# Zero-filled 128-partition tiles for the 16-token block of a hybrid four-layer kernel

## The chip, the core and the metric

The kernel runs on one core of one Trainium2 chip. A core has five engines with instruction queues of their own: TensorE (PE; its weight loads are listed as PEld), VectorE (DVE), ScalarE (ACT), GpSimd (POOL) and SyncE (SP, which issues the transfers here). They share two memories of 128 partitions: SBUF for the data and PSUM, into which PE writes. The metric is the time of one execution in microseconds (us); lower is better.

## The reference

A sequence of 1040 tokens (16 learned "meta" tokens, then 1024 input tokens, each with 1024 features) goes through four layers: attention, mLSTM, HGRN2, attention. Each layer is

```python
u = rmsnorm(h, norm_gain[i])
y = branch(u, ...)          # attention (0, 3), mLSTM (1), HGRN2 (2)
h = h + where(valid, y, 0)
```

and the output is `h` without the meta tokens. The reference fills up the front to a whole block of 128 with tokens that are not valid, so its first block holds only the 16 meta tokens. The attention is causal within a window of 128 tokens, has 16 heads with 4 key/value heads, and a learned sink per head in its softmax. The other two branches are recurrences that carry a state per head from block to block:

```python
# mLSTM, a block of 128, per head (8 heads, keys of 128, values of 256)
qk  = (q @ k.T) * exp(D - m_t)
num = w_inter * (q @ C) + qk @ v
C   = w_old * C + (w_s * k).T @ v
# HGRN2, per head (8 heads, keys and values of 128)
o   = (q * exp(A)) @ S + att @ v
S   = exp(A_last) * S + (k * exp(A_last - A)).T @ v
```

All of it is float32.

## The kernel before

The tokens lie along the free dimension in most places (`x`, `uh`, `ul` are 128 features by 1040 tokens for each of eight feature groups). The padding of the reference is not computed: the sequence is cut into nine blocks, block 0 with the 16 meta tokens (`NMETA`) and eight of 128. Function `blk(b)` gives a block's first token and its length.

**The big projections.** A float32 product is made of three products of F32R tiles: a number is split into a high and a low part (`split`), and high by high, high by low and low by high are added up in PSUM. `proj` (line 231) makes projections with tokens in columns, in chunks of 400, 384 and 256 tokens; `proj_v` (lines 276 and 280) makes values with tokens in rows, a block at a time; `proj_out` (line 325) is the output projection. Beside these, each layer has a mixer made of small products, most of them plain float32 products, which PE executes in two passes (a group "x2" in the timeline).

**Layer 0 and 3, attention** (`layer_a`). The work is cut into units: four pairs of query tiles, nine blocks (eight in layer 3, where block 0 is not needed), two halves. A unit has three steps. `S_step` makes the scores on PE (lines 723, 724), puts the sinks behind them on POOL (line 728), and makes the softmax on DVE, ACT and POOL in tile `Sm` (lines 731 to 737). `T_step` transposes `Sm` on PE (line 749) and splits the result into `Ph` on ACT (line 751) and `Pl` on DVE (line 752). `V_step` multiplies by the values (line 768). The steps of one unit are put two units apart (`T_LAG`, `V_LAG`): in the order on PE, V_step of a unit, T_step of the unit two later and S_step of the one four later follow each other. `Sm`, `Ph` and `Pl` have two buffers each.

**Layer 1, mLSTM** (`layer_b`). Per head and block, `s1` makes the scores and the weighted keys (tiles `w`, `kw`, lines 997 and 1003), `s2` the output (line 1010, and from block 1 on line 1012 with the carried state), normalised into `hn` on ACT (line 1018), `s3` the update of the state (line 1024), and `s4` transposes `hn` (line 1038) back to tokens in columns. The values come from `put_v` (lines 243 to 246), which copies them from PSUM to a tile of 128x258; for block 0 it adds two parts, which `proj_v` left in rows 0 to 15 and 32 to 47. A column of ones stands behind the values (`g.memset` at line 972).

**Layer 2, HGRN2** (`layer_c`). Per head there are five regions: block 0 alone, then pairs of blocks. `level` and `level_mm` make the decayed scores (lines 1236 to 1262), `tail0` adds them up to `att`, `tail1` transposes the weighted keys (line 1312) into `kT` (line 1314), `states` updates the state (line 1322), `tail2` makes the output (lines 1343 and 1345).

In block 0 these products use 16 partitions: for instance `W["kw", b][:cn]` by `V[:cn, :257]` in `s3`, with `cn` = 16.

**What sets the order.** The order on PE is written out by hand: every layer makes lists of steps with a cost, `weave` mixes the list of a mixer with the list of projections in proportion to their costs, and the result is executed as listed. PE's order is thus the same whatever the other engines do. Their order is made by the framework: it takes the instructions as the program emits them, with the mixers' steps raised by 40 places (`hi`, `PRIO`), and lists them on each engine by priority and by the times that its own estimates give. It also sets the waits, and it gives a tile a buffer when the first instruction that touches it is listed.

The functions that the change touches, with the callers:

Of the kernel before, what the change touches and what calls it, by code (L numbers as in the profile page):

```python
# [15 lines left out]
P = 128  # L16
# [97 lines left out]
def hybrid_kernel(ctx: ExitStack, tc: tile.TileContext, ins, out, layers=(0, 1, 2, 3)):  # L114
# [125 lines left out]
    def put_v(V, acc, b, cn):  # L240

        if b == 0:
            s.copy(V[:cn, :256], acc[32 : 32 + cn, :256])
            v.tensor_tensor(V[:cn, :256], V[:cn, :256], acc[:cn, :256], op=ALU.add)
        else:
            s.copy(V[:cn, :256], acc[:cn, :256])
# [232 lines left out]
    def layer_a(i, j, first, last, fin, scale=None):  # L479
# [217 lines left out]
        def mixers():  # L697


            def S_step(w):  # L700
# [16 lines left out]
                S = psum("pm", 2).rearrange("p (u k) -> p u k", u=2)  # L717
                w["Sm"] = Sm = mix.tile([P, 2, 257], F32, tag="Sm", name=nm("Sm"), bufs=2)
                st, den = small(2), small(2)
                sinks = []  # L720
# [19 lines left out]
            def T_step(w):  # L740
# [4 lines left out]
                w["Ph"] = Ph = R["mix"].tile([P, 2, 2, P], F32R, tag="Ph", name=nm("Ph"), bufs=2)  # L745
                w["Pl"] = Pl = R["mix"].tile([P, 2, 2, P], F32R, tag="Pl", name=nm("Pl"), bufs=2)
                for ki, (kb, ko, _) in enumerate(kbs):
                    for u in range(2):
                        pe.transpose(pt[:kn, ki, u, :nq], Sm[:nq, u, ko : ko + kn], ident[:nq, :nq])  # L749
                src, h, l = (z[:kn, : len(kbs), :, :nq] for z in (pt, Ph, Pl))  # L750
# [3 lines left out]
            def V_step(w):  # L754
                b, kbs, hh, pair = w["b"], w["kbs"], w["hh"], w["pair"]
                q0, nq = blk(b)
                kn = NMETA if b == 0 else P
                grp = [z for z in GROUPS if b in z][0]
# [7 lines left out]
                for ki, (kb, _, _) in enumerate(kbs):  # L766
                    for part in ("Ph", "Pl"):
                        pe.matmul(po[:, :, q0 - g0 : q0 - g0 + nq], V[pair // 2, kb][:kn, P * hh : P * hh + P],  # L768
                                  w[part][:kn, ki, :, :nq], start=(ki == 0 and part == "Ph"),
                                  stop=(ki == len(kbs) - 1 and part == "Pl"))  # L770
# [87 lines left out]
    def layer_b(i, j, fin):  # L858
# [116 lines left out]
        def mixer(h):  # L975
# [8 lines left out]
            def s1(b):  # L984
# [10 lines left out]
                s.activation(E[:cn, :cn], E[:cn, :cn], AF.Exp)  # L995
                W["W", b] = w = mix.tile([P, P], F32, tag="W", name=nm("W"), bufs=2)
                v.tensor_tensor(w[:cn, :cn], E[:cn, :cn], pq[:cn, :cn], op=ALU.mult)
                if b:
                    W["qw", b] = qw = mix.tile([P, P], F32, tag="qw", name=nm("qw"), bufs=2)
                    v.tensor_tensor(qw, q[:, cs], R["wb"][:, cs], op=ALU.mult)  # L1000
                if b < NB - 1:
                    W["kw", b] = kw = mix.tile([P, P], F32, tag="kw", name=nm("kw"), bufs=2)
                    s.activation(kw[:cn], pq[:cn, 128:256], AF.Identity, scale=E[:cn, cn - 1 : cn])

            def s2(b):
# [3 lines left out]
                num = psum("po", 1)  # L1009
                pe.matmul(num[:cn, :257], W["W", b][:cn, :cn], V[:cn, :257], start=True, stop=(b == 0))  # L1010
                if b:
# [4 lines left out]
                v.reciprocal(den[:cn], den[:cn])  # L1016
                W["hn", b] = hn = mix.tile([P, 256], F32, tag="hn", name=nm("hn"), bufs=2)
                s.activation(hn[:cn], num[:cn, :256], AF.Identity, scale=den[:cn])

            def s3(b):  # L1020
                mix = R["mix"]
                c0, cn = blk(b)
                pc = psa()
                pe.matmul(pc[:, :257], W["kw", b][:cn], R["v", h, b][:cn, :257], start=True, stop=True)  # L1024
                Cn = mix.tile([P, 258], F32, tag="C", name=nm("C"), bufs=2)
# [7 lines left out]
            def s4(b):  # L1033
                c0, cn = blk(b)
                cs = slice(c0, c0 + cn)
                pt = psum("pt", 1)
                for c in range(2):
                    pe.transpose(pt[:, c * P : c * P + cn], W["hn", b][:cn, c * P : c * P + P], ident[:cn, :cn])
                for c in range(2):
                    v.tensor_copy(R["h", h, c][:, cs], pt[:, c * P : c * P + cn])  # L1040
# [90 lines left out]
    def layer_c(i, j, fin):  # L1131
# [80 lines left out]
        def mixer(h):  # L1212
# [56 lines left out]
            def tail0(r):  # L1269
# [10 lines left out]
                if r == 0:  # L1280
                    att = R["mix"].tile([16, 16], F32, tag="att0", name=nm("att0"), bufs=1)
                    v.tensor_reduce(att, t6[:16, 0, f0:, :w].rearrange("p l t -> p t l"),
                                    axis=mybir.AxisListType.X, op=ALU.add)
# [22 lines left out]
            def tail1(r):  # L1306
                c0, cn = geom(r)
                bn = min(cn, P)
                pt = psum("pt", 1)
                W["kT", r] = kT = R["mix"].tile([P, 256], F32, tag="kT", name=nm("kT"), bufs=1)  # L1310
                for b in range(len(REGIONS[r])):
                    pe.transpose(pt[:bn, P * b : P * b + P], W["kA", r][:, P * b : P * b + bn], ident)
# [3 lines left out]
            def states(r):  # L1316
# [3 lines left out]
                for b in blocks:  # L1320
                    cn = blk(REGIONS[r][b])[1]
                    pe.matmul(pc[:, P * b : P * b + P], W["kT", r][:cn, P * b : P * b + P],
                              R["v", h // 2, REGIONS[r][b]][:cn, vs], start=True, stop=True)
                for b in blocks:
# [7 lines left out]
            def tail2(r, b):  # L1332
# [9 lines left out]
                att = W["att", r] if r == 0 else W["att", r][:, b, :]  # L1342
                pe.matmul(W["po"][:, oc], V[:cn, vs], att, start=True, stop=(r == 0))
                if r:
# [263 lines left out]
```

## Time and profile before

| | |
|---|---|
| time, median of 3 runs | 2616.81 us (2613.16 to 2617.46) |
| the profiled execution: time | 2619.49 us |
| the profiled execution: span, first to last instruction | 2617.7 us |
| mean granted clock of PE in it | 0.993 |
| instructions | 54451 |
| DVE busy | 1961.7 us (75%) |
| ACT busy | 1696.7 us (65%) |
| POOL busy, instructions | 238.8 us (9%), 488 |

A view by line lists groups of equal instructions with their busy time and mean duration. The timeline lists single instructions in order of time: start, duration, engine, line, operation, the tile written and the tiles read, the shape. For PE the shape begins with the loaded weights: "16*128 16x257" means weights of 16 partitions by 128 columns and 257 columns streamed through 16 partitions. A bracket at the end names idle time of the engine before this instruction, and what ended it; "issue" is a wait for nothing that the profile shows. A view by windows gives the busy time of PE, PEld, DVE, ACT and POOL in stretches of the span, with the number of instructions in brackets. Matmuls overlap: the next one begins before the end of the one before, so their durations add up to more than the time that passes, and their starts are what to read.

### The profile page before, as it was taken

Reading aid. Unit: us, or ns where it says so; the run is one execution under the profiler, and the core shown is the slowest. Engines: PE = TensorE matmul, PEld = TensorE weight load, DVE = VectorE, ACT = ScalarE, POOL = GpSimd, SP = SyncE. Lnnn points to the kernel's source line nnn. Section 1 sums busy time; section 2 is a strip of 40 time slices with the busy share of each in tenths; the row PEclk is TensorE's granted clock in tenths of the full one; section 3 lists DMA queues with packets and bytes.
Section 4 is the critical chain, followed back from the end, with each engine's and each line's share of the span. In section 5 each row is a group of like instructions: output and inputs, shape, how many; then the busy total and the mean of one; then the engine's idle time right before and its main releaser. Section 6 shows DMA issues by size and latency. Waiting matters only on the chain.

```text
span 2617.7 us, 54451 instructions
## 1 busy us (share of the span) xinstructions
PE 2571.5 (98%) x20446; PEld 2493.2 (95%) x20446; DVE 1961.7 (75%) x5290; ACT 1696.7 (65%) x4434; POOL 238.8 (9%) x488
## 2 busy tenths in 40 slices
PE   8999999999999999999999999999999999999999
PEld 7899989999999999999999999999999999999999
DVE  6797888885747464646565688989887978887896
ACT  7766767575555555455545757878685857767772
POOL 0321221000000000000000000100000000321330
PEclk8999999999999999999999999999999999999999
DMA  4123112021111111111111101111110112212112
GB/s 149 53 67 98 54 54 71 21 67 57 41 58 41 50 44 53 41 57 41 55 43 50 53 30 42 34 34 34 34 42 30 38 51 88 59 47 84 55 41 77
DMA packets 86058, 140.21 MB, mean 54 GB/s; under 512 B 12425, under 2 KB 39186, under 8 KB 85794
## 3 DMA queue, kind: packets, MB, share of 16 engines
q1 hardware_dynamic: 85794, 136.73, 17.0%
q8 instruction: 161, 2.64, 0.4%
q14 instruction: 103, 0.84, 0.1%
HBM read 121.83 MB, written 4.27 MB: 48 GB/s over the span
## 4 chain that ended last, share of the span: by engine, by line
PE 75%; DVE 8%; ACT 4%; DMA 1%; issue 1%; POOL 0%; SPq 0%; DVEq 0%; ACTq 0%; POOLq 0%
PE pj L231 37%; PE pj L325 15%; PE pj L280 10%; PE po L768 1%; PE pt L749 1%; PE po L1010 1%; PE pa L1024 1%; PE po L1012 1%; PE pj L276 1%; PE pm L1262 1%; DVE wl L196 1%; PE pm L723 1%; DMA cs<-in_rope 1%; PE pm L724 1%; DVE Sm L731 1%
## 5 line engine op out<-in xcount | busy, mean ns | idle before, releaser
L231 PE MATMUL pj<-uh,wh 128*128 128x256 f32 (+2 forms) x2688 | 917.0, 341 | 7.2 <-ACT uh L400 6.7
L231 PE MATMUL pj<-ul,wh 128*128 128x256 f32 (+2 forms) x2688 | 866.5, 322 | 0.3
L231 PE MATMUL pj<-uh,wl 128*128 128x256 f32 (+2 forms) x2688 | 866.5, 322 | 0.0
L231 PEld LDWEIGHTS pj<-uh,wh 128*128 128x128 f32 x2688 | 510.1, 190 | 24.4 <-issue 9.3
L231 PEld LDWEIGHTS pj<-ul,wh 128*128 128x128 f32 x2688 | 510.6, 190 | 6.0 <-DVE ul L196 0.9
L231 PEld LDWEIGHTS pj<-uh,wl 128*128 128x128 f32 x2688 | 509.4, 190 | 0.0
L196 DVE TENSOR_TENSOR wl<-wr,wh 128x512 fp32r<-128x512 f32 (+1 forms) x338 | 232.5, 697 | 52.0 <-ACT wh L195 48.8
L195 ACT CAST wh<-wr 128x512 fp32r<-128x512 f32 (+1 forms) x338 | 202.7, 613 | 99.4 <-PE pj L325 33.4
L325 PE MATMUL pj<-yh,wh 128*128 128x384 f32 (+2 forms) x768 | 253.8, 330 | 9.9 <-DVE x L328 8.0
L328 DVE TENSOR_TENSOR x<-x,pj 128x384 f32<-128x384 f32 (+2 forms) x480 | 234.9, 509 | 33.3 <-PE pj L325 32.0
L325 PE MATMUL pj<-yh,wl 128*128 128x384 f32 (+2 forms) x768 | 246.2, 321 | 0.0
L325 PE MATMUL pj<-yl,wh 128*128 128x384 f32 (+2 forms) x768 | 246.1, 320 | 0.0
L280 PE MATMUL pj<-wh,uh 128*128 128x256 f32 (+1 forms) x768 | 232.7, 303 | 0.0
L280 PE MATMUL pj<-wl,uh 128*128 128x256 f32 (+1 forms) x768 | 216.4, 282 | 0.0
L280 PE MATMUL pj<-wh,ul 128*128 128x256 f32 (+1 forms) x768 | 216.0, 281 | 0.0
L734 ACT ACTIVATE Sm<-Sm,s 128x257 f32<-128x257 f32 (+2 forms) x272 | 130.9, 483 | 88.9 <-DVE s L731 84.5
L737 POOL TENSOR_TENSOR Sm<-Sm,s 128x512 f32<-128x512 f32 (+2 forms) x136 | 142.4, 1047 | 421.0 <-DVE s L736 407.4
L457 ACT ACTIVATE t<-t 128x384 f32<-128x384 f32 (+2 forms) x240 | 117.8, 491 | 82.3 <-DVE t L456 80.0
L325 PEld LDWEIGHTS pj<-yh,wh 128*128 128x128 f32 x768 | 144.9, 189 | 14.1 <-DVE x L328 9.7
L195 ACT CAST yh<-r 128x384 fp32r<-128x384 f32 (+2 forms) x120 | 56.9, 479 | 153.1 <-PE pj L325 136.9
L280 PEld LDWEIGHTS pj<-wh,uh 128*128 128x128 f32 x768 | 144.7, 188 | 2.2
L280 PEld LDWEIGHTS pj<-wl,uh 128*128 128x128 f32 x768 | 144.9, 189 | 1.9
(287 smaller groups left out, 5408.7 us busy)
## 6 DMA issues: line engine op xcount, KB each, us to landing
wr<-in_b_win SPq DMA_DIRECT2D x124, 256.0 KB, 3.0
wr<-in_a_win SPq DMA_DIRECT2D x80, 256.0 KB, 2.9
wr<-in_c_win SPq DMA_DIRECT2D x64, 256.0 KB, 2.7
wr<-in_a_wout SPq DMA_DIRECT2D x32, 256.0 KB, 2.9
wr<-in_b_wout SPq DMA_DIRECT2D x32, 256.0 KB, 2.8
t<-t SPq DMA_DIRECT2D x100, 48.0 KB, 2.0
cs<-in_rope SPq DMA_DIRECT2D x11, 400.0 KB, 3.4
cs<-in_rope SPq DMA_DIRECT2D x11, 384.0 KB, 3.7
```

Of the source, the lines that this page charges most:

```text
L195: s.copy(h, src)
L196: v.tensor_tensor(l, src, h.bitcast(F32), op=ALU.subtract)
L231: pe.matmul(acc[:, :cn], a[:, k, :], b[:, k, c0 : c0 + cn], start=(k == 0 and i == 0), stop=(k == KT - 1 and i == 2))
L276: pe.matmul(acc[:48, :nc], um[0][:, k, :], m[:, kk, :], start=(k == 0 and m is wh), stop=(k == KT - 1 and m is wl))
L280: pe.matmul(acc[:cn, :nc], a[:, k, c0 : c0 + cn], m[:, kk, :], start=(k == 0 and j == 0), stop=(k == KT - 1 and j == 2))
L325: pe.matmul(acc[:, :cn], a[:, k, mc], b, start=(k == 0 and i == 0), stop=(k == 1 and i == 2))
L328: v.tensor_tensor(x[:, m, c0 : c0 + cn], x[:, m, c0 : c0 + cn], acc[:, :cn], op=ALU.add)
L457: s.activation(a[:, :cn], a[:, :cn], AF.Exp)
L723: pe.matmul(S[:nq, u, :kw], q[:, qb], kh[:, kb], start=True, stop=False)
L724: pe.matmul(S[:nq, u, :kw], q[:, qb], kl[:, kb], start=False, stop=True)
L734: s.activation(Sm[:nq, u, : nk + 1], Sm[:nq, u, : nk + 1], AF.Exp, scale=-1.0, bias=st[:nq, u : u + 1], accum_out=den[:nq, u : u + 1])
L737: g.tensor_tensor(Sm[:nq, :, :nk], Sm[:nq, :, :nk], den[:nq].rearrange("p (u c) -> p u c", c=1).to_broadcast([nq, 2, nk]), op=ALU.mult)
```

## The change

For block 0, the tiles that feed the small products are filled with zeros by GpSimd before their 16 used partitions (or columns) are written, and the products then read all 128 partitions. These are `V` of layers B and C (in `put_v`), `Sm`, `Ph` and `Pl` of layer 0, `w`, `kw` and `hn` of layer B, and `att` and `kT` of layer C (`att` grows from 16 to 128 partitions). `V` of layer 0 had its zeros already (line 679). The transpositions of `Sm` and `hn` use the whole 128x128 identity, and so stream 128 columns in place of 16. The number of columns of the other products is unchanged; `W` in `s2` keeps its 16 columns of weights. The added rows are zeros, so the sums stay what they were.

```diff
     def put_v(V, acc, b, cn):
         if b == 0:
+            g.memset(V, 0.0)
             s.copy(V[:cn, :256], acc[32 : 32 + cn, :256])
...
                 w["Sm"] = Sm = mix.tile([P, 2, 257], F32, tag="Sm", name=nm("Sm"), bufs=2)
+                if b == 0:
+                    g.memset(Sm[:, :, :NMETA], 0.0)
...
+                if b == 0:
+                    for z in (Ph, Pl):
+                        g.memset(z[:, 0, :, :NMETA].bitcast(F32), 0.0)
                 for ki, (kb, ko, _) in enumerate(kbs):
                     for u in range(2):
-                        pe.transpose(pt[:kn, ki, u, :nq], Sm[:nq, u, ko : ko + kn], ident[:nq, :nq])
+                        pe.transpose(pt[:kn, ki, u, :], Sm[:, u, ko : ko + kn], ident)
...
-                        pe.matmul(po[:, :, q0 - g0 : q0 - g0 + nq], V[pair // 2, kb][:kn, P * hh : P * hh + P],
-                                  w[part][:kn, ki, :, :nq], start=(ki == 0 and part == "Ph"),
+                        pe.matmul(po[:, :, q0 - g0 : q0 - g0 + nq], V[pair // 2, kb][:, P * hh : P * hh + P],
+                                  w[part][:, ki, :, :nq], start=(ki == 0 and part == "Ph"),
...
                 W["W", b] = w = mix.tile([P, P], F32, tag="W", name=nm("W"), bufs=2)
+                if b == 0:
+                    g.memset(w[:, :cn], 0.0)
...
                     W["kw", b] = kw = mix.tile([P, P], F32, tag="kw", name=nm("kw"), bufs=2)
+                    if b == 0:
+                        g.memset(kw, 0.0)
...
-                pe.matmul(num[:cn, :257], W["W", b][:cn, :cn], V[:cn, :257], start=True, stop=(b == 0))
+                pe.matmul(num[:cn, :257], W["W", b][:, :cn], V[:, :257], start=True, stop=(b == 0))
...
                 W["hn", b] = hn = mix.tile([P, 256], F32, tag="hn", name=nm("hn"), bufs=2)
+                if b == 0:
+                    g.memset(hn, 0.0)
...
-                pe.matmul(pc[:, :257], W["kw", b][:cn], R["v", h, b][:cn, :257], start=True, stop=True)
+                pe.matmul(pc[:, :257], W["kw", b], R["v", h, b][:, :257], start=True, stop=True)
...
-                    pe.transpose(pt[:, c * P : c * P + cn], W["hn", b][:cn, c * P : c * P + P], ident[:cn, :cn])
+                    pe.transpose(pt[:, c * P : c * P + P], W["hn", b][:, c * P : c * P + P], ident)
...
-                    att = R["mix"].tile([16, 16], F32, tag="att0", name=nm("att0"), bufs=1)
-                    v.tensor_reduce(att, t6[:16, 0, f0:, :w].rearrange("p l t -> p t l"),
+                    att = R["mix"].tile([P, 16], F32, tag="att0", name=nm("att0"), bufs=1)
+                    g.memset(att, 0.0)
+                    v.tensor_reduce(att[:16], t6[:16, 0, f0:, :w].rearrange("p l t -> p t l"),
...
                 W["kT", r] = kT = R["mix"].tile([P, 256], F32, tag="kT", name=nm("kT"), bufs=1)
+                if r == 0:
+                    g.memset(kT[:, :P], 0.0)
...
-                    pe.matmul(pc[:, P * b : P * b + P], W["kT", r][:cn, P * b : P * b + P],
-                              R["v", h // 2, REGIONS[r][b]][:cn, vs], start=True, stop=True)
+                    pe.matmul(pc[:, P * b : P * b + P], W["kT", r][:, P * b : P * b + P],
+                              R["v", h // 2, REGIONS[r][b]][:, vs], start=True, stop=True)
...
-                pe.matmul(W["po"][:, oc], V[:cn, vs], att, start=True, stop=(r == 0))
+                pe.matmul(W["po"][:, oc], V[:, vs], att, start=True, stop=(r == 0))
```

More of the change, by code (lines that the diff above doesn't have):

```diff
@@ L756, in V_step @@
                 q0, nq = blk(b)
-                kn = NMETA if b == 0 else P
                 grp = [z for z in GROUPS if b in z][0]
```

## The prediction

> **What bounds the kernel now.** I read the page first: the busy line, then the chain that ended last.
>
> ```profile
> span 2617.7 us, 54451 instructions
> PE 2571.5 (98%) x20446; PEld 2493.2 (95%) x20446; DVE 1961.7 (75%) x5290; ACT 1696.7 (65%) x4434; POOL 238.8 (9%) x488
> PE 75%; DVE 8%; ACT 4%; DMA 1%; issue 1%; POOL 0%; SPq 0%; DVEq 0%; ACTq 0%; POOLq 0%
> ```
>
> PE is busy 98% of the span and carries 75% of the chain; it stands still for only 2617.7 - 2571.5 = 46.2 us. Its order is written out by hand, so a product that takes PE 0.4 us less lets everything behind it on PE start 0.4 us earlier, unless a wait takes it back. POOL works 9% of the time. So the question is what a 16-row product costs PE beside a 128-row one.
>
> Busy time can't answer this, because matmuls overlap. I use the timeline of PE and measure a detour: the big projection (line 231) runs at an even beat, a small product is put between two of its matmuls, and the detour is what the beat loses. First the state product s3 of layer B (line 1024), once with 16 rows (block 0) and once with 128 (a later block). Columns: start us, duration, engine, line, tiles, shape.
>
> ```profile
> 561.79 0.34 PE L231 MATMUL pj<-uh,wl 128*128 128x400 f32 x1
> ...
> 562.34 0.34 PE L231 MATMUL pj<-uh,wl 128*128 128x400 f32 x1
> 562.61 0.70 PE L1024 MATMUL pa<-v,kw 16*128 16x257 f32 x2
> ...
> 563.52 0.34 PE L231 MATMUL pj<-ul,wh 128*128 128x384 f32 x1
> ...
> 568.58 0.34 PE L231 MATMUL pj<-uh,wl 128*128 128x384 f32 x1
> 568.75 0.59 PE L1024 MATMUL pa<-v,kw 128*128 128x257 f32 x2
> ...
> 569.30 0.28 PE L231 MATMUL pj<-ul,wh 128*128 128x256 f32 x1
> 569.42 0.28 PE L231 MATMUL pj<-uh,wl 128*128 128x256 f32 x1
> ```
>
> The beat is 0.18 us at 400 columns (three starts in 562.34 - 561.79 = 0.55) and 0.12 at 256 (569.42 - 569.30); 0.18 also at 384. Between the matmul before the product and the second one after it lie two beats. With 16 rows: 563.52 - 562.34 - 2 x 0.18 = 0.82 us. With 128 rows: 569.30 - 568.58 - 0.18 - 0.12 = 0.42 us. Same 257 columns, an eighth of the work, twice the time. The weight loads (PEld) show why:
>
> ```profile
> 562.61 0.29 PEld L1024 LDWEIGHTS pa<-v,kw 16*128 16x128 f32 x2 [0.26 <-ACT s L1014]
> 563.23 0.19 PEld L231 LDWEIGHTS pj<-uh,wh 128*128 128x128 f32 x1 [0.33 <-issue]
> ...
> 568.58 0.36 PEld L1024 LDWEIGHTS pa<-v,kw 128*128 128x128 f32 x2
> ```
>
> The 128-row load starts at 568.58, 0.17 us ahead of its own matmul and under the one before. The 16-row load starts with its matmul at 562.61 after the loader stood idle 0.26 us, and so does the load after it, after 0.33 us. Going into a 16-row product and coming out of it, PE loads nothing ahead.
>
> **The change part by part.** Every edited product occurs eight times in block 0: eight heads in B and in C, four pairs by two halves in layer 0; layer 3 leaves block 0 out.
>
> *s3 of B*, 16x257 to 128x257: 8 x (0.82 - 0.42) = 3.2 us off PE.
>
> *s2 of B* (line 1010) goes from 16 rows and 16 columns of weights to 128 rows, but still 16 columns:
>
> ```profile
> 559.43 0.34 PE L231 MATMUL pj<-uh,wl 128*128 128x400 f32 x1
> 559.70 0.60 PE L1010 MATMUL po<-v,W 16*16 16x257 f32 x2
> ...
> 560.52 0.34 PE L231 MATMUL pj<-ul,wh 128*128 128x400 f32 x1
> ```
> ```profile
> 1856.67 0.26 PEld L1262 LDWEIGHTS pm<-X 128*16 128x16 f32 x8 [0.26 <-issue]
> ```
>
> Its detour is 560.52 - 559.43 - 0.36 = 0.73. No row shows its new shape. The ends are 0.42 (full product, above) and 0.73 (no gain). The nearest row is the load in layer C with 128 rows and 16 columns, also ordinary f32: it stands idle 0.26 before, as the 16-row ones do. I take no gain, and keep 8 x 0.31 = 2.5 us as the other end.
>
> *s4 of B* (line 1038), two transpositions, 16 columns streamed to 128:
>
> ```profile
> 694.31 0.28 PE L231 MATMUL pj<-uh,wl 128*128 128x256 f32 x1
> 694.52 0.29 PE L1038 MATMUL pt<-ident,hn 16*128 16x16 f32 x2
> ...
> 695.03 0.34 PE L231 MATMUL pj<-ul,wh 128*128 128x400 f32 x1
> ```
> ```profile
> 747.04 0.34 PE L231 MATMUL pj<-uh,wl 128*128 128x400 f32 x1
> 747.22 0.38 PE L1038 MATMUL pt<-ident,hn 128*128 128x128 f32 x2
> ...
> 747.61 0.34 PE L231 MATMUL pj<-ul,wh 128*128 128x384 f32 x1
> ```
>
> 0.72 - 0.12 - 0.18 = 0.42 before, 0.57 - 0.36 = 0.21 after, though eight times the columns pass: 8 x 0.21 = 1.7 us.
>
> *Layer C, states and tail2* (lines 1322, 1343):
>
> ```profile
> 1623.85 0.34 PE L231 MATMUL pj<-uh,wl 128*128 128x400 f32 x1
> 1624.12 0.48 PE L1322 MATMUL pa<-v,kT 16*128 16x128 f32 x2
> ...
> 1624.83 0.34 PE L231 MATMUL pj<-ul,wh 128*128 128x400 f32 x1
> ...
> 1625.55 0.34 PE L231 MATMUL pj<-uh,wl 128*128 128x400 f32 x1
> 1625.83 0.39 PE L1343 MATMUL po<-att,v 16*128 16x16 f32 x2
> ...
> 1626.43 0.34 PE L231 MATMUL pj<-ul,wh 128*128 128x384 f32 x1
> ```
> ```profile
> 1685.89 0.28 PE L231 MATMUL pj<-uh,wl 128*128 128x256 f32 x1
> 1686.00 0.61 PE L1322 MATMUL pa<-v,kT 128*128 128x128 f32 x4
> ...
> 1686.57 0.28 PE L231 MATMUL pj<-ul,wh 128*128 128x256 f32 x1
> ```
>
> The last block holds two full products in 0.68 - 0.24 = 0.44, so 0.22 each. States: 0.98 - 0.36 = 0.62 to 0.22, 8 x 0.40 = 3.2 us. tail2: 0.88 - 0.36 = 0.52 to at most 0.22 (it streams 16 columns, not 128; I take 0.22), 8 x 0.30 = 2.4 us.
>
> *Layer 0, V_step* (line 768), two products in F32R:
>
> ```profile
> 160.03 0.33 PE L231 MATMUL pj<-uh,wl 128*128 128x384 f32 x1
> 160.29 0.28 PE L768 MATMUL po<-Ph,v 16*128 16x32 f32 x1
> ...
> 160.84 0.28 PE L231 MATMUL pj<-ul,wh 128*128 128x256 f32 x1
> ```
>
> 0.81 - 0.18 - 0.12 = 0.51. A full F32R product of even 256 columns takes a beat of 0.12, two take 0.24: 8 x 0.27 = 2.2 us.
>
> *Layer 0, T_step* (line 749): two transpositions as in s4, but out of 16 columns of weights. Between nothing and s4's 0.21; I take half, 8 x 0.1 = 0.8 us.
>
> Sum on PE: 3.2 + 0 + 1.7 + 3.2 + 2.4 + 2.2 + 0.8 = 13.5 us.
>
> *The memsets.* 12 for V, 8 for Sm, 16 for Ph and Pl, 24 for w, kw and hn, 16 for att and kT: 76.
>
> ```profile
> L679 POOL MEMSET v<- 128x258 f32 x4 | 1.3, 314 | 0.3 <-POOLq L1599 0.3
> ```
> ```profile
> 352.49 0.33 POOL L728 COPY Sm<-cons 16x2 f32<-16x2 f32 x1 [3.82 <-PE pt L749]
> ```
> ```profile
> 353.78 0.27 DVE L731 CUSTOM_DVE_ANT_0 Sm<-pm,masks,cons 16x16 f32<-16x16 f32 x1
> ```
>
> None is larger than 128x258, so 76 x 0.314 = 24 us at most, on an engine that idles 2617.7 - 238.8 = 2379 us. What counts is the new wait. A memset waits for its buffer's last reader, then holds the first writer: on ACT the copies into V, kw, hn, Ph and kT, on DVE the reductions into Sm and att and the product into w. Behind a held one, its engine's whole queue stands. The tightest cover is Sm: its buffer comes free with a transposition just ahead of the scores on PE. The copy of the sinks on POOL waits for the same event, starts at 352.49, and the first reduction begins 1.29 us later; a memset of at most 0.31 ahead of it leaves about 1 us. For Ph and Pl the last reader is the V_step just ahead of the transposition on PE, and their own reader comes two units later; for the others it is in an earlier block or head. So I cost them nothing; without cover each kind costs 8 x 0.31 = 2.5 us. PE itself waits for nothing new that comes late.
>
> Not all of 13.5 us will arrive:
>
> ```profile
> 1610.00:2115.00 505.00, 498.73 (x6677) 475.72 (x6676) 432.67 (x1427) 385.20 (x1094) 47.41 (x128) 1.00 0.13 38
> ```
>
> In layer C, PE (first figure) waits 6.3 of 505 us and DVE (third) works 86%. Some of C's 5.6 us only makes PE reach such a wait sooner; I take off 0.7, and keep 0 to 3. Result: 12.8 us. The profiled execution took 2617.7 us of span and 2619.49 in all, 2.7 above the median 2616.81 and within 0.11% of it; I set the sum against the median: 2604.0 us.
>
> **The rivals.**
>
> *Rows don't matter.* If the small product's cost came from its place and not from its 16 rows, filling it changes nothing and the transpositions get longer: 0.38 instead of 0.29 for a pair, 16 pairs, 1.4 us, so 2618. The two s3 rows speak against it: same line, columns and neighbours, 0.82 against 0.42. The Trainium skill, TensorE: Matmul & The Clock Gate, section "Why this matters for your kernels", says this in its row on small K: a single matmul with K=32 takes the same time as one with K=128. Taken alone it would give this 2618; the trace disagrees, as a full-height product in this stream hides its weight load and a 16-row one does not.
>
> *s2 gains too*, if 16 columns of weights cost nothing: 2.5 us more, 2601.5. The idle 0.26 before the load of line 1262 is against it.
>
> *Waits take half.* If DVE or ACT set the pace beside PE, half of the sum goes, 6.7 us: 2610. For it: DVE's 86%. Against: PE is busy 98.8% in that stretch (498.73 of 505).
>
> *Slower: the planner rearranges ACT and DVE.* Only PE's order is fixed; the framework orders the rest by its own estimates, and 76 new instructions shift these. A copy put behind the wrong neighbour makes PE wait. The place is layer 0, layer C and layer 3, where PE waits already. To end over 0.2% slower, waits must grow by 13.5 + 5.2 = 18.7 us, 40% of the 46.2 there are. If they grow by half, 23 us, the time is 2626. Against it: the memsets need an engine that is nearly always free.
>
> **How the numbers follow.** Main case 0.66 (2604, its own range 2600 to 2608), s2 too 0.08 (2601.5), half lost 0.10 (2610), rows don't matter 0.05 (2618), slower 0.11 (2626). A measurement tells 0.2%, 5.2 us, from no change: faster, below 2611.6, are the first three less a little, 0.82; same 0.07; slower 0.11. The range 2598 to 2613 holds the first three: below, all terms at their best ends (13.5 + 2.5 + 0.9 = 16.9, less nothing) and 2 us for the runs' spread; above, the half-lost case with the same spread.
>
> **What would show it.** After the change the 16-row forms are gone from lines 749, 768, 1010, 1024, 1038, 1322 and 1343. The loads of 1024 and 1322 in block 0 start ahead of their matmuls without idle time; s3's detour falls to 0.42, states to 0.22, s4's to 0.21; the load of 1010 still stands idle 0.26. POOL rises by at most 24 us. I am wrong if those detours stay, if PE's idle time grows from 46 us by more than 10, or if ACT or DVE show waits on POOL memsets with PE waiting behind them.

## The result, and the profile after

The changed kernel takes 2608.6 us (2605.71 to 2616.01) against 2616.0 (2613.16 to 2619.85): a ratio of 0.9979, with a 95% interval of 0.9970 to 0.9988. That is 5.5 us of 2616, faster by just over what can be told from no change, where 12.8 were forecast. The head of its page:

```profile
span 2605.6 us, 54402 instructions
PE 2554.9 (98%) x20446; PEld 2490.2 (96%) x20446; DVE 1963.1 (75%) x5290; ACT 1691.7 (65%) x4434; POOL 245.2 (9%) x564
PE 67%; DVE 12%; ACT 8%; DMA 2%; issue 2%; SPq 0%; POOL 0%; DVEq 0%; ACTq 0%; POOLq 0%
```

POOL has the 76 memsets, for 6.4 us. PE's idle time grew from 46.2 to 50.7 us, and PE's share of the chain that ended last fell from 75% to 67%, in favour of DVE and ACT: first signs that waits took something back. The products themselves got cheaper as forecast. The same places in the timeline of the changed kernel, s2, s3 and s4 of layer B, then states and tail2 of layer C, then V_step of layer 0:

```profile
552.55 0.34 PE L231 MATMUL pj<-uh,wl 128*128 128x400 f32 x1
552.82 0.61 PE L1019 MATMUL po<-v,W 128*16 128x257 f32 x2
...
553.64 0.34 PE L231 MATMUL pj<-ul,wh 128*128 128x400 f32 x1
...
555.48 0.34 PE L231 MATMUL pj<-uh,wl 128*128 128x400 f32 x1
555.66 0.59 PE L1035 MATMUL pa<-v,kw 128*128 128x257 f32 x2
...
556.26 0.34 PE L231 MATMUL pj<-ul,wh 128*128 128x384 f32 x1
...
686.97 0.28 PE L231 MATMUL pj<-uh,wl 128*128 128x256 f32 x1
687.09 0.38 PE L1049 MATMUL pt<-ident,hn 128*128 128x128 f32 x2
...
687.49 0.34 PE L231 MATMUL pj<-ul,wh 128*128 128x400 f32 x1
...
1612.95 0.34 PE L231 MATMUL pj<-uh,wl 128*128 128x400 f32 x1
1613.13 0.39 PE L1336 MATMUL pa<-v,kT 128*128 128x128 f32 x2
...
1613.54 0.35 PE L231 MATMUL pj<-ul,wh 128*128 128x400 f32 x1
...
1614.28 0.35 PE L231 MATMUL pj<-uh,wl 128*128 128x400 f32 x1
1614.46 0.29 PE L1357 MATMUL po<-att,v 128*128 128x16 f32 x2
...
1614.86 0.34 PE L231 MATMUL pj<-ul,wh 128*128 128x384 f32 x1
...
155.23 0.34 PE L231 MATMUL pj<-uh,wl 128*128 128x384 f32 x1
155.41 0.18 PE L773 MATMUL po<-Ph,v 128*128 128x32 f32 x1
...
155.75 0.28 PE L231 MATMUL pj<-ul,wh 128*128 128x256 f32 x1
```

And T_step of layer 0, whose weights keep 16 columns:

```profile
141.88 0.34 PE L231 MATMUL pj<-uh,wl 128*128 128x400 f32 x1
142.06 0.38 PE L755 MATMUL pt<-ident,Sm 128*16 128x128 f32 x2
...
142.47 0.35 PE L231 MATMUL pj<-ul,wh 128*128 128x400 f32 x1
```
```profile
141.88 0.27 PEld L755 LDWEIGHTS pt<-ident,Sm 128*16 128x16 f32 x2
```

Read as in the prediction, the detours are 0.73 (s2, no gain), 0.42 (s3), 0.22 (s4), 0.23 (states), 0.22 (tail2), 0.22 (V_step) and 0.23 us (T_step, 0.34 before). PE's saving is 8 x (0.40 + 0.20) = 4.8 us in layer B, 8 x (0.39 + 0.30) = 5.5 in C and 8 x (0.29 + 0.11) = 3.2 in layer 0. So it was made, and lost elsewhere. (T_step is worth a second look: with 128 rows its load starts 0.18 us ahead of its products, without idle time, and the detour is that of the full transpositions of s4, although its weights are only 16 columns wide.)

Where it was lost can be read because PE's order is the same in both kernels: every projection matmul has its counterpart. Four of them, before and then after (ends of layer 0 and of B, start and end of C):

```profile
519.95 0.29 PE L280 MATMUL pj<-wl,uh 128*128 128x272 f32 x1
...
1514.97 0.34 PE L231 MATMUL pj<-uh,wl 128*128 128x384 f32 x1
...
1571.98 0.34 PE L231 MATMUL pj<-uh,wh 128*128 128x400 f32 x1
...
2118.06 0.34 PE L231 MATMUL pj<-uh,wh 128*128 128x384 f32 x1
```
```profile
513.07 0.29 PE L281 MATMUL pj<-wl,uh 128*128 128x272 f32 x1
...
1504.25 0.34 PE L231 MATMUL pj<-uh,wl 128*128 128x384 f32 x1
...
1561.28 0.34 PE L231 MATMUL pj<-uh,wh 128*128 128x400 f32 x1
...
2105.07 0.34 PE L231 MATMUL pj<-uh,wh 128*128 128x384 f32 x1
```

The lead is 6.88, 10.72, 10.70 and 12.99 us. Layer B won 3.8 of its 4.8 us, layer C 2.3 of 5.5. In layer B every head gave its saving, and the rest went at two waits that the kernel before does not have: 0.5 us at s2 of a later block, which now waits for the state C (line 1040), also in only_b below; and 0.4 us at its end, where two loads of weights (line 1094) wait for DVE. The waits of PE in layer B, of which the kernel before has none:

```profile
PE po L1021 <- DVE C L1040: 0.3, 1, 0.3
```

The 6.88 us at the end of layer 0 are mostly not the change's: the shown execution of the kernel before ran with a granted clock of 0.91 in its first 80 us and 0.83 from 240 to 260 (the changed one 0.96 and 1.00), and an execution whose layer 0 is that of the kernel before, but which was spared that from 240 us on (only_c below), stands 1.1 us ahead of the changed kernel there. Of this 0.5 us was there at 60 us, before the first V_step, so layer 0 lost about 0.6. Behind layer C the lead falls from 12.99 us to 12.1 at the end of the two executions: layer 3, which the change does not touch, gave back 0.9.

### The profile page after: what moved, and what is told of

Same layout as the page of the kernel before. It is cut to its first block, busy times and chain, and to the rows that moved or that the text cites. A ratio compares the mean times of both kernels' runs of the same rounds, so it can differ in the third digit from the quotient of the medians.

```text
span 2605.6 us, 54402 instructions
## 1 busy us (share of the span) xinstructions
PE 2554.9 (98%) x20446; PEld 2490.2 (96%) x20446; DVE 1963.1 (75%) x5290; ACT 1691.7 (65%) x4434; POOL 245.2 (9%) x564
## 4 chain that ended last, share of the span: by engine, by line
PE 67%; DVE 12%; ACT 8%; DMA 2%; issue 2%; SPq 0%; POOL 0%; DVEq 0%; ACTq 0%; POOLq 0%
PE pj L231 31%; PE pj L326 15%; PE pj L281 10%; PE po L773 1%; PE po L1019 1%; PE pt L755 1%; PE po L1021 1%; DVE wl L196 1%; PE pa L1035 1%; DVE Sm L734 1%; ACT wh L195 1%; ACT X L1249 1%; ACT Sm L737 1%; DVE X L1247 1%; PE pj L277 1%
```

## Experiments

All versions compute the whole result. Products called unread below are added work whose results go nowhere. sweep, shift_before, shift_after, nudge_before, phase_after and phase_p_once were executed once, for their traces, and have no row here.

| version | median us | before beside it | ratio, 95% interval |
|---|---|---|---|
| memsets_only | 2617.21 | 2613.4 | 1.0011 (1.0002 to 1.0021) |
| only_a (layer 0) | 2614.12 | 2613.4 | 0.9999 (0.9990 to 1.0008) |
| only_b | 2608.2 | 2613.4 | 0.9985 (0.9973 to 0.9997) |
| only_c | 2611.27 | 2613.4 | 0.9989 (0.9980 to 0.9998) |
| cols | 2610.25 | 2614.82 | 0.9983 (0.9973 to 0.9992) |
| kt_after | 2608.25 | 2614.82 | 0.9974 (0.9964 to 0.9984) |
| p_once | 2615.21 | 2614.82 | 1.0004 (0.9994 to 1.0013) |
| bc_cols | 2606.13 | 2614.05 | 0.9965 (0.9953 to 0.9977) |
| bc_cols_kt | 2605.67 | 2614.05 | 0.9966 (0.9954 to 0.9979) |
| best | 2624.89 | 2612.9 | 1.0046 (1.0032 to 1.0061) |
| nudge_after | 2607.46 | 2612.98 | 0.9975 (0.9965 to 0.9985) |
| best2 | 2602.11 | 2612.98 | 0.9961 (0.9949 to 0.9973) |

**The parts alone.** First the zeros without the taller products, then the whole edit in one layer at a time.

```diff
 # memsets_only: every memset stays, the products read 16 rows again, for instance
-pe.matmul(pc[:, :257], W["kw", b], R["v", h, b][:, :257], ...)
+pe.matmul(pc[:, :257], W["kw", b][:cn], R["v", h, b][:cn, :257], ...)
 # only_a, only_b, only_c: memsets and tall products in layer 0, B or C; the rest as before
```

> All 76 memsets as in the change, but every product and transposition of block 0 keeps its 16 rows. Theory 1 (the memsets and the waits that they add are free, the missing gain was taken by waits on ACT and DVE that PE reaches sooner): no change, 2614 to 2618 us, and the detours stay at 0.82 (s3), 0.73 (s2), 0.42 (s4), 0.62 (states), 0.52 (tail2). Theory 2 (the memsets, or the planner's new order around them, cost what is missing): 3 to 6 us slower than before, 2619 to 2622.

> The change in layer 0 alone: 8 x (0.29 + 0.11) = 3.2 us on PE. Theory 1: the waits of layer 0 take about half, 1.5 us faster, within 1 us of noise. Theory 2: the new order takes all of it or more: no change or up to 2 us slower.

> The change in layer B alone: 8 x (0.40 + 0.21) = 4.9 us on PE, where PE hardly waits. Theory 1: all of it arrives, 4.5 to 5 us faster, 2611. Theory 2: the planner's new order on DVE and ACT (it moves about a hundred instructions each) costs 1 to 3 us of it in layers C and 3, so 2 to 4 us faster.

> The change in layer C alone. The planner's order on DVE and ACT is the same as in the kernel before. PE's own saving there is 8 x (0.40 + 0.30) = 5.6 us. Theory 1 (PE reaches existing waits sooner and gives back more than half): 2 to 3 us faster, with the waits for kT (line of its copy on ACT) and for att longer than before. Theory 2 (a new order of ACT and DVE took it): with the order unchanged nearly all of it arrives, 5 us faster.

Layer B gives 3.9 us, layer C 2.9, layer 0 nothing, and the zeros alone cost 2.9, each by its interval within some 2.5 us either way (the zeros: 0.5 to 5.5). So two terms were wrong: the zeros are not free, and layer C keeps about half.

**Layer C: the wait behind the products.** The waits of PE from 1560 to 2120 us (reader, releaser, us in all, times, longest) in the kernel before, the changed one and only_c:

```profile
PE pa L1322 <- ACT kT L1314: 2.8, 6, 0.9
```
```profile
PE pa L1336 <- ACT kT L1328: 4.1, 7, 1.0
```
```profile
PE pa L1349 <- ACT kT L1341: 5.3, 8, 1.3
```

In only_c the order on DVE and ACT is that of the kernel before, to the instruction. PE is earlier by the saving, ACT's copy of kT comes when it came, and 2.5 of 5.5 us turn into waiting for it. By the starts of the projection matmuls all eight heads give their saving in only_c, and PE loses 2.9 us at six products that wait for kT and 0.45 at one that waits for att of POOL. The copy stands in ACT's queue behind casts of weights and activations of other heads, so it does not come sooner when PE does. The states products were then put later, by

```diff
-KT_LAG, ATT_LAG = 900.0, 600.0
+KT_LAG, ATT_LAG = 2500.0, 600.0
```

> The changed kernel, with KT_LAG 2500 instead of 900: in layer C the states products come later behind their transposition, by 1600 columns of projection, some 0.75 us. Theory 1 (half of layer C's saving went because PE reached the wait for ACT's copy kT sooner): the waits of the states products fall from 4.1 us (7 times) to under 1, layer C gets 2 to 3 us shorter, and the ratio falls to about 0.997. Rival (layer C's saving was lost to the memsets' own time on POOL, or to DVE as a whole, which works 86% there): the kT waits go, but others grow by as much, and the ratio stays within 0.0005 of 0.9979.

```profile
PE po L1372 <- DVE S L1356: 3.6, 4, 1.8
PE pm L1285 <- DVE X L1262: 2.9, 3, 1.7
```

The kT waits are gone. In their place PE waits 3.6 us for the states S of DVE, which now come late for the next product, and 0.8 us more for X. Neither theory holds whole: kT was the wait that took the saving, and behind it stood the next. The gain over the changed kernel, 0.0005, is inside the intervals.

**Which heights pay.** The prediction's two open prices were s2's, with 128 rows and 16 columns of weights, and the height from which a product is cheap.

```diff
+SWEEP = 16, 32, 48, 64, 80, 96, 112, 128   # by head, block 0: rows of s3 and s4, columns of s2
-pe.matmul(pc[:, :257], W["kw", b], R["v", h, b][:, :257], ...)
+kr = cn if b else SWEEP[h]
+pe.matmul(pc[:, :257], W["kw", b][:kr], R["v", h, b][:kr, :257], ...)
```

> The changed kernel, but in block 0 of layer B the height is swept over the eight heads: head 0 holds 16 rows (s3, s4) and 16 columns of weights (s2), then 32, 48, 64, 80, 96, 112, and head 7 holds 128. Nothing is left out of the result. Theory 1 (the array works in whole tiles of 32, 64 or 128 rows, and only a full-height tile lets the loader run ahead): the detour of s3 is 0.82 us up to 64 rows and 0.43 from 80 on; s4 0.42 and then 0.22; s2, which always has 128 rows now, shows 0.73 up to 64 columns of weights and 0.43 from 80 on. Rival (every height under 128 drains): 0.82, 0.42 and 0.73 in seven heads, and only the last is cheap. Second rival (cost falls in proportion with rows): s3 falls evenly from 0.82 to 0.43, about 0.06 for each step. The time is no measure here; PE's work should lie about 2 to 5 us above the changed kernel.

s3 of the heads with 64 and with 80 rows:

```profile
948.99 0.34 PE L238 MATMUL pj<-uh,wl 128*128 128x384 f32 x1
949.26 0.70 PE L1048 MATMUL pa<-v,kw 64*128 64x257 f32 x2
...
950.16 0.34 PE L238 MATMUL pj<-ul,wh 128*128 128x384 f32 x1
...
1082.44 0.34 PE L238 MATMUL pj<-uh,wl 128*128 128x384 f32 x1
1082.62 0.60 PE L1048 MATMUL pa<-v,kw 80*128 80x257 f32 x2
...
1083.23 0.34 PE L238 MATMUL pj<-ul,wh 128*128 128x384 f32 x1
```

1.17 - 0.36 = 0.81 us at 64 rows, 0.79 - 0.36 = 0.43 at 80. The heads up to 64 rows give 0.81 to 0.83, those from 80 on 0.42 or 0.43; s4 falls from 0.47 to 0.19, and s2 by columns of weights from 0.77 to 0.43, all between 64 and 80. There is a step and no slope. The Trainium skill, TensorEngine Tiling (Array Packing), says in section "Key Properties" that a change of tiling mode drains TensorE, and its section "Available Configurations" has modes of 32, 64 or 128 rows and columns; a step between 64 and 80 agrees with that. T_step does not fit for the columns: its transpositions with 128 rows and 16 columns of weights show no such price. So narrow weights are shown to cost in s2, a plain f32 product of two passes, and not in every product; why, no run shows. The page gives no price; here it is about 0.4 us for s3 and 0.3 for s2 and s4.

```diff
-g.memset(w[:, :cn], 0.0)
+g.memset(w, 0.0)
-pe.matmul(num[:cn, :257], W["W", b][:, :cn], V[:, :257], ...)
+pe.matmul(num[:, :257], W["W", b], V[:, :257], ...)
```

> The changed kernel, with s2 of block 0 given all 128 columns of weights too (the memset fills the whole tile W, and the product writes 128 rows of PSUM of which 16 are read). The order on DVE, ACT and SP is that of the changed kernel. Theory 1 (the narrow weights kept the drain): the detour of s2 falls from 0.73 to 0.43 us, eight times, 2.4 us off PE in layer B, and the time falls by 1.5 to 2.5 us, to a ratio of 0.9970 to 0.9974 against the kernel before. Rival (s2 is slow for its place, or for waiting on W): the detour stays at 0.73, the ratio stays at 0.9979.

s2's detour fell to 0.41 to 0.44 in all eight heads, and layer B got 2.1 us shorter than in the changed kernel. The time shows no clear part of it (0.9983 against 0.9979, inside the intervals): in this execution the kT waits at the end of layer C took it back (1.62 us instead of 1.02, and 2.22 instead of 0.93). The detour is settled, its worth in time is not told by this comparison.

**Layer 0: which cause.** In executions with the new zeros in layer 0, PE loses about 1.0 us at the first V_step (76 us) and 1.4 to 2.6 us at 165 to 178, against only_c. First, V_step alone was filled, with zeros that are written once, so that the planner's order stays:

```diff
+for tag in ("Ph", "Pl"):
+    R[tag, 0] = [mix.tile([P, 1, 2, 16], F32R, name=nm(tag + "0")) for _ in range(2)]
+    for z in R[tag, 0]:
+        g.memset(z.bitcast(F32), 0.0)
...
-w["Ph"] = Ph = R["mix"].tile([P, 2, 2, P], F32R, tag="Ph", ...)
+w["Ph"] = Ph = R["Ph", 0][w["hh"]] if b == 0 else R["mix"].tile([P, 2, 2, P], F32R, tag="Ph", ...)
...
-bufs=12 if w < 8 else 4
+bufs=1 if w < 2 else 8 if w < 8 else 4
```

> The kernel before, with V_step of layer 0 alone filled to 128 rows, and its zeros written once: the block-0 tiles Ph and Pl get four small buffers of their own, set to zero at the start of the layer, so 4 memsets and not 16. (To make room, the small(1) and small(2) pools have 1 and 8 buffers instead of 12; that alone changes the order on no engine.) SP's order of transfers is that of the kernel before, and 8 instructions of DVE and 8 of ACT change places, where the version with all of layer 0's edits changed 54 and 38 and moved 3 transfers. Theory 1 (layer 0's saving was eaten by the planner's new order, which the memsets of each unit brought): the detour of V_step falls by 0.28 us, eight times, and all of it arrives: 2.2 us, ratio 0.9989 to 0.9994. Rival (layer 0 has slack on PE, so a saving there never arrives, whatever the order): ratio 0.9997 to 1.0003, with PE idle longer by 2.2 us in layer 0.

The expectation failed: 1.0004 (0.9994 to 1.0013). But the two losses come apart. T_step's wait, in only_c, memsets_only and p_once:

```profile
168.03 0.63 PE L763 MATMUL pt<-ident,Sm 128*128 128x128 f32 x4 [0.22 <-DVE s L741]
```
```profile
171.18 0.63 PE L763 MATMUL pt<-ident,Sm 128*128 128x128 f32 x4 [1.22 <-DVE s L741]
```
```profile
168.14 0.63 PE L763 MATMUL pt<-ident,Sm 128*128 128x128 f32 x4 [0.19 <-DVE s L744]
```

With the old order the 1.2 us wait is gone; with the zeros of every unit, which moved 20 places on DVE and 15 on ACT, it is there, and no PE wait names a memset. POOL executes no memset from 148 to 262 us in memsets_only. What differs there is what DVE, which has no idle time, executes between `Pl` and the second reduction of the softmax (until 171.0 us, where T_step's wait ends). In memsets_only:

```profile
169.08 0.56 DVE L482 TENSOR_TENSOR t<-t,t 128x384 f32<-128x384 f32 x1
170.02 0.55 DVE L483 TENSOR_TENSOR r<-r,t 128x384 f32<-128x384 f32 x1
```

In only_c both come behind that reduction. The other loss stayed in p_once. The cast that V_step's values wait behind, and V_step itself, in only_c and in p_once:

```profile
72.30 0.62 ACT L201 CAST wh<-wr 128x512 fp32r<-128x512 f32 x1 [0.62 <-DMA wr<-in_a_win]
75.84 0.36 PE L782 MATMUL po<-Ph,v 16*128 16x32 f32 x1 [4.33 <-DVE v L694]
```
```profile
73.46 0.62 ACT L201 CAST wh<-wr 128x512 fp32r<-128x512 f32 x1 [1.58 <-DMA wr<-in_a_win]
77.00 0.36 PE L782 MATMUL po<-Ph,v 128*128 128x32 f32 x1 [5.32 <-DVE v L699]
```

A weight transfer of 256 KB lands 1 us later. In the DMA view of the changed kernel from 71 to 72 us stands what came between (packets, MB, share of the 16 DMA engines):

```profile
q8 instruction: 1, 0.02, 6.1%
```

This queue has 161 packets of 16 KB in the run, one for 254 matmuls and weight loads of PE (2 x 20446 / 161), and they come with PE's progress: I read them as loads of PE's own program. In the kernels without zeros in layer 0 this one comes after 358 passes of PE, behind V_step's wait; with them after 352 or 353, ahead of it. Six versions moved it, by unread products at PE's start that change nothing else of note:

```diff
+for z in [psum("pj", 3) for _ in range(8)]:       # shift_before: 1 product each, shift_after: 2
+    pe.matmul(z[:, :P], ones, ones, start=True, stop=True)
 # nudge_before, nudge_after: 5 in all; phase_after, phase_p_once: 56 in all; one column each
+    pe.matmul(z[:, :1], ones, ones[:, :1], start=True, stop=True)
```

> The kernel before, with eight products of the tile of ones with itself added at the very start of PE's program, where PE waits for its first data (their results are read by nobody); they lengthen PE's program by some 32 instructions and nothing else (on DVE 3 and on ACT 6 instructions of the first normalisation change places). Theory 3 (a 16 KB load of PE's own program, which comes once in some 256 instructions, holds up the weight transfer that layer 0's first V_step hangs on, in those kernels where a few added PE instructions move the load from just behind that wait, at about 76.7 us, to just ahead of it, at about 71): here the load comes at 69 to 71 us, the transfer lands about 1 us later, and the wait of the first V_step grows from 4.3 to 4.6 us (kernels without edits in layer 0) to 5.2 to 5.7 (kernels with them). Rival (the memsets on POOL, or the planner's order, lengthen that wait): none of them is here, so the wait stays at 4.3 to 4.6.

> The changed kernel with sixteen such products, some 64 instructions, at the start of PE's program. Theory 3: PE's program load moves from 71 us to about 65 to 67, ahead of the weight transfer, and the wait of layer 0's first V_step shrinks from 5.4 to about 4.4 us. Rival (memsets or the planner's order): they are all still here, and the wait stays at 5.2 to 5.7.

> The kernel before, with five products of one column (read by nobody) at the start of PE's program, 10 passes on PE; the order on DVE, ACT, POOL and SP is unchanged. In the kernel before, PE's program load comes after 358 passes, just behind the wait of layer 0's first V_step (which is pass 357), in the changed kernel after 353, just ahead of it. Theory 3 (the load holds up the weight transfer): the load comes at 69 to 71 us, the transfer of the weights that ACT casts behind it takes 4.4 to 4.7 us from issue to cast instead of 3.6, and the wait of the first V_step is 5.2 to 5.7 us. Rival (memsets or order): neither is changed, the wait stays at 4.3 to 4.6.

> The changed kernel with 56 such products, 112 passes, which put the load some 16 passes later in PE's order than in the changed kernel, so behind the first V_step again. Theory 3: the load comes at 77 to 80 us, the transfer takes about 3.6 us, the wait of the first V_step is 4.3 to 4.6 us. Rival: the wait stays at 5.2 to 5.7. The second part of the loss (PE waiting about 1 us longer for T_step and for the scores at 168 to 175 us) stays in both: that is the planner's order, which is the changed kernel's here.

> The version with V_step alone filled and zeros written once, with the same 56 products. Theory 3: the wait of the first V_step falls from 5.3 to 4.3 to 4.6 us, and between 60 and 160 us PE comes to lie 0.5 us (two V_steps by 0.28) ahead of the version with layer 0 as before, instead of about 0.5 behind. Rival: the wait stays, and PE stays behind.

> The changed kernel with five one-column products (read by nobody) at the start of PE's program; the order on the other engines is unchanged. Theory 3: the program load moves from 71.1 us to 68.5 to 70, ahead of the data of the weight transfer, the wait of the first V_step falls from 5.4 to 4.4 to 4.7 us, and the time by about 1 us, to a ratio near 0.9975; PE's longer waits at 168 to 175 us, by the planner's order, stay. Rival (that wait is the memsets' or the order's): it stays at 5.2 to 5.7 and the ratio at 0.9979.

From the timelines of SP and ACT: the transfer before the last one (to the next issue), the last one (issue to cast), and V_step's wait, in us:

| version | load at | before the last | last | wait |
|---|---|---|---|---|
| only_c | 76.7 | 4.08 | 3.57 | 4.33 |
| p_once | 70.9 | 4.07 | 4.54 | 5.32 |
| changed kernel | 71.1 | 4.09 | 4.50 | 5.39 |
| nudge_before | 69.1 | 4.08 | 3.71 | 4.47 |
| shift_before | 66.0 | 4.82 | 3.85 | 5.58 |
| shift_after | 65.0 | 4.98 | 3.83 | 5.62 |
| phase_after | 92.8 | 4.11 | 3.84 | 4.37 |

The load slows the transfer whose data are moving, by 0.7 to 1.0 us, whichever it is. Both shifts put it on the transfer before, so shift_after's expectation failed with the mechanism at work; nudge_before put it between two transfers, and there it costs nothing, also against its expectation. Where it comes behind the wait the wait is short: 4.37 us in phase_after and 4.61 in phase_p_once, with all their zeros. In nudge_after it came at 71.9 us, 0.2 us ahead of the issue of the last transfer, and the wait was 4.78. Over all twenty traces, the last transfer takes 4.28 to 4.76 us where the load falls into it and 3.57 to 3.97 where it does not. That the load is the cause of this part is shown in both directions: shift_before lengthens the wait without a memset, and phase_after shortens it with all of them. What it is worth in time is read from the wait alone: nudge_after's 0.9975 against the changed kernel's 0.9979 is inside the intervals.

**Versions that keep what pays.**

bc_cols is layers B and C of the change with the s2 of cols, and layer 0 as before; bc_cols_kt adds the first line below; best adds to bc_cols the V_step of p_once and 56 unread products, best2 five:

```diff
-KT_LAG, ATT_LAG = 900.0, 600.0
+KT_LAG, ATT_LAG = 1700.0, 600.0
...
-    for _ in range(7):
-        pe.matmul(z[:, :1], ones, ones[:, :1], start=True, stop=True)
+for z in [psum("pj", 3) for _ in range(8)][:5]:
+    pe.matmul(z[:, :1], ones, ones[:, :1], start=True, stop=True)
```

> The change in layers B and C alone (layer 0 as before), with s2's 128 columns of weights as in the earlier run. PE's own saving by the detours: 4.7 in B, 2.4 for s2, 5.6 in C. Theory 1 (B's savings arrive, half of C's is lost to the kT waits, layer 0's edits bring nothing): 4.7 + 2.4 + 2.6 = 9.7 us, ratio 0.9957 to 0.9969, faster than the changed kernel (0.9979). Rival (PE's savings are lost further on whatever they are, since layers C and 3 hang on DVE and ACT): ratio 0.9975 or more, no better than the changed kernel.

> The same with KT_LAG 1700 instead of 900 (with 2500 the kT waits went and waits for the states S of DVE came in their place, so this is half way). Theory 1: kT waits of layer C halve, to about 2 us or less, the S waits stay under 2, and the time is 0 to 2 us below the run without it. Rival (the waits in layer C only change their names): equal within 1 us, or slower.

> All that has paid so far: layers B and C filled, s2 with 128 columns of weights, and in layer 0 V_step alone, with its zeros written once and the 56 products at the start. PE's savings: 7.1 in B, 5.6 in C, 2.2 in layer 0. Theory (B arrives, C to less than half, layer 0 arrives once the load is off the transfer, but for 0.5 at the wait at 248 us): 6.3 to 7.1, 1.5 to 2.6, and about 1.5, together 9.3 to 11.2 us, ratio 0.9957 to 0.9964. Rival (layer 0 never gives anything): 0.9965 to 0.9970, as with B and C alone.

> Layers B and C filled, s2 with 128 columns of weights, V_step of layer 0 alone with its zeros written once, and the five one-column products. Theory (layer 0's saving arrives once the load is off the transfer, but for about 0.9 at the waits at 166 and 248 us): the wait of the first V_step is 4.4 to 4.7 us, and the time lies 1 to 1.5 us below the version with B and C alone (ratio 0.9965), at 0.9958 to 0.9962. Rival (layer 0 gives nothing): 0.9964 or more.

bc_cols takes 2606.13 us; KT_LAG 1700 adds nothing (waits for kT fell from 5.2 to 1.7 us, those for X rose from 2.1 to 3.9 and for S to 1.2). best was spoilt by its own device: its 56 one-column products take 24 us and hold PE's first matmul back by 18, as in phase_after:

```profile
1.05 24.05 PE L491 MATMUL pj<-ones 128*128 128x1 f32 x112 [1.05 <-DVE consts L392]
```

With five products best2 takes 2602.11 us, ratio 0.9961, the lowest of all. Against only_c, whose layer 0 is the old one, its PE gains 3.1 us between 60 and 520 us, as much as V_step's 2.3 and more, though 0.5 of it is a shorter wait at 248 us (1.06 against 1.61). By time alone this is not shown: the interval of best2 overlaps that of bc_cols (0.9965), so what speaks against the rival, that layer 0 gives nothing, is this one pair of traces.

```profile
span 2598.6 us, 54408 instructions
PE 2552.8 (98%) x20456; PEld 2492.6 (96%) x20456; DVE 1961.8 (75%) x5290; ACT 1692.3 (65%) x4434; POOL 244.4 (9%) x544
```

## Why the prediction was right and wrong

The sign and the mechanism on PE were right. The price lies in the form of the product and not in its place: that rival fell at every detour but s2's, which had been forecast to stay and fell when its columns were filled too (cols). The terms of the 13.5 us came out within 0.02 us a product, s2 without gain included.

Wrong was what stands behind the sum: the two terms for what the rest of the kernel takes back. By layers the forecast was 4.9 us in B, 5.6 - 0.7 = 4.9 in C and 3.0 in layer 0, together 12.8; measured were 3.8, 2.3 and about -0.6. *The memsets*: "So I cost them nothing." On POOL they do cost nothing, 6.4 us on an idle engine. But the zeros alone made the kernel 2.9 us slower: they changed the planner's order of DVE and ACT in layer 0 (1.4 us at 165 to 178 in memsets_only, up to 2.6 with the taller products), and in the kernels that have them a load of PE's program falls onto a transfer (1.0 us), which no part of the prediction considered. In the profiled execution of memsets_only 0.9 us more went at 80 to 90 us, where the granted clock was 0.50 until 82 us. The rival of the planner had named layer 0, but as a cause of 18.7 us or nothing; its small form happened and, with the load, ate all of layer 0's 3.2.

*Waits in layer C*: "I take off 0.7, and keep 0 to 3." About 3.2 of 5.5 us went, in only_c most of it at the wait for kT. I had taken 6.3 us of idle time in the stretch as slack that small savings would hardly touch. But an idle time is what is left of a race: where PE waits for kT already, all that it wins ahead of that wait is lost there. My test, PE's idle time growing by more than 10 us, was too coarse for a sum of 13: it grew by 4.5.

*Layer B* was given no waits at all, and lost 1.0 us, 0.5 at the wait for C and 0.4 at the loads of line 1094.

The sum by what was measured: B 3.8, C 2.3 and layer 0 about -0.6 give 5.5 us, as the ratio does. That it meets the ratio so exactly is luck: the ratio's interval is 3.1 to 7.8 us, and the 0.9 us that layer 3 gave back in these executions are not in the sum. That the planner's order, and not the zeros themselves, makes the waits at 165 to 178 us is argued from p_once, and from memsets_only, where no memset runs in that stretch and DVE's order differs; no version had the new order without the zeros. In the changed kernel itself the idle time for kT grew by only 1.3 us; where the rest of layer C's loss went there was not followed.

## What to carry to other kernels

Between full f32 matmuls, make small products taller than 64 rows, and for plain f32 products also wider than 64 columns of weights (T_step's transpositions did not need that); zeros are a cheap way. Then look at the next wait behind each product that got cheaper: where PE waits already, much of the saving is lost until the releaser comes sooner too (in layer C here, more than half). And compare the order on the other engines before and after a harmless addition: the order, and the place where a program load falls, can cost as much as the edit wins.

## What the runs showed of the hardware

One load of 16 KB of PE's program in the middle of a 256 KB transfer makes it 0.7 to 1.0 us later, and a handful of PE instructions decides which transfer it meets. A product of one column is not free: 0.21 us a pass (24.05 / 112) at the start of the program. The projection's 400 columns right behind take 0.33 us there (starts at 25.45 and 25.78 us in best), not the 0.18 of the later stream, so the 0.21 can't be set beside the 0.18. And PE's clock can lose time after a wait: in the stretch from 240 to 260 us, with a wait of 1.69 us in the kernel before and of 1.07 in the changed one (columns: us, busy time of PE, PEld, DVE, ACT, POOL, granted clock, DMA share, GB/s):

```profile
240.00:260.00 20.00, 18.31 (x80) 14.70 (x79) 11.92 (x24) 13.14 (x28) 0.00 (x0) 0.83 0.54 152
```
```profile
240.00:260.00 20.00, 18.93 (x118) 16.76 (x117) 11.90 (x25) 16.10 (x38) 0.00 (x0) 1.00 0.47 136
```

Such drops came with long waits in some executions and not in others (only_c: a wait of 1.61 us and a clock of 1.00), at some 3 us in the kernel before, so sums over a whole execution were read with care and the stretches one by one.
